# Splitting the SSD chunks by head group, and a new order of attention fill and output projection, in a hybrid layer kernel

## The chip, the cores and the metric

The kernel runs on one core of a Trainium2 chip. The metric is the device time of one execution in microseconds (us). Engines are named as the profile names them: PE is the matrix engine and PEld its weight loads, DVE the vector engine, ACT the scalar (activation) engine, POOL the general-purpose engine, and SP the engine that here only issues DMAs. Each engine works through its own instructions in order and waits on semaphores for the others. PE adds into PSUM, which is kept in banks of 128 x 512 float32; everything else lies in SBUF (128 partitions) or, between stages, in DRAM.

## The reference: what is computed

One layer over 2048 positions with model width 1024, in float32. Two mixers read the same normalised input, and one projection takes both back:

```
proj = rmsnorm(x) @ w_in              # q, k, v, z_sb, z_ssd, xBC, dt
q, k = rmsnorm per head (16 heads x 64)
z    = q k^T * scale                  # strictly causal
w    = exp(log_sigmoid(z) + sum over later keys of log_sigmoid(-z))
y_sb = rmsnorm((w @ v) * silu(z_sb), sb_norm_w)

xBC  = silu(causal_depthwise_conv(xBC, 4 taps))   # 12 blocks of 128 channels
y    = ssd_chunked(x*dt, dt*a, B, C)  # 16 heads, 2 B/C groups, chunks of 128
y_ssd = rmsnorm((y + D*x) * silu(z_ssd), ssd_norm_w)

out  = x + concat(y_sb, y_ssd) @ w_out
```

In the chunked scan each chunk of 128 positions makes a product inside the chunk (`C B^T` under a decay matrix `exp(a_t - a_s)`), one with the state carried in, and a new state `carry`. The heads of group 0 read B and C of group 0, those of group 1 of group 1; the groups share nothing else, and a chunk needs the state of the chunk before.

## The kernel before

**Stages.** The sequence is worked in two halves of 1024 positions (`H` = 0, 1), because a half of the normalised input fits in SBUF. In the order of the program: loading and splitting the input (to about 30 us), the four conv blocks of half 0 (to 145), SSD chunks and the SSD branch's gate projections of half 0 (to 385), attention for the queries of half 0 (to about 1010) and of half 1 (to about 2080), the conv blocks of half 1 (to 2195), its SSD chunks (to 2335), the output projection of the attention branch, called part 0 here (`br` = 0, to 2506), and of the SSD branch, part 1 (to 2702).

**Matmuls.** To keep float32 accuracy every operand is split into a rounded high part and the rest (`hh`, `hl`, `wh`, `wl`, `yh`, `yl`), and a product is made of three matmuls. A 128 x 512 block of a projection over the depth of 1024 is 8 x 3 = 24 matmuls of 512 columns. PSUM has eight banks under four tags: `z` 2, `t` 2, `av` 1, `pj` 3.

**SSD (`ssd`).** `conv(sg)` makes three of the twelve channel blocks: 144 matmuls in all, then for each block and half of 512 positions a copy from PSUM to `u` (ACT), the first tap with the bias (ACT), three taps (DVE, `scalar_tensor_tensor`), `Sigmoid` (ACT, into a buffer of `wk`) and a product (POOL). Blocks 0 to 2 come before block 3, which is called fourth here. `chunk(c)` makes both head groups of one chunk: transposes of x to `t`, `xd` (DVE) and `xdd` (POOL), the B/C product and its mask `cb` (DVE), for each of two quarters of heads a decay tile `wk`, also called `lm` (a broadcast DMA, four `Relu` and one `Exp` on ACT, a product with `cb` on POOL), the matmuls of L422 (inside the chunk) and L426 (with `carry`), two DVE operations into `ea` and one into x, the state matmul L434 and two DVE operations on `carry`. The gate projections `gates(wz, j, q)` are 24 matmuls each and depend on none of this. In half 0 all 16 blocks stand behind the chunks in the program; in half 1 the last four stand between chunks 0 and 1, chunks 2 and 3, and the rest (`CS` = (0, 2, 4)), together with the loading and splitting of `w_out` for part 0 (`load_wo`); the other twelve were made during attention.

**Attention (`attention`).** Sixteen segments per half: pairs of heads `p` and query halves `q` of 512 positions. For a segment, `stage_a` projects q, k and v and normalises q and k by rows, `stage_b` transposes them and makes the value differences `vd` (each value row less the one before), which the scan form of the stick-breaking weights needs, and `gate` the attention's gate. They are the fill: Python generators of small steps, from which a planner takes one whenever the inner loop of the current segment has saved up `UNIT` = 0.55 us of due time. That inner loop runs z (L610, L611), two ACT operations, the scan on DVE (L619), transposes (L628), a split and the value matmuls (L645, L646). `fill_for(n)` sets the fill's order while segment n runs.

**Output projection (`out_part`).** For each of 16 tiles of 128 positions: load the residual `res`, the branch `yr` and, in part 1, its gate `zr`; in part 1 two POOL products and a `Sigmoid` (L748 to L750); squares and their sum over the depth (`sq`, `sqs`, then a `ones` matmul, L757); a product with the norm's weight (POOL, L761); the split into `yh` (ACT, L762) and `yl` (DVE, L763); 48 matmuls, 24 for each half of 512 columns (L769 to L771); and the scaling by the row's norm with the residual added (L772), then a store. `yr` and `zr` have three buffers, `res` two.

**Order.** The program is written for a scheduler that places an instruction by its priority in the program and by when it can start, so that each engine's order isn't the order of the code; tiles of a pool wait for the last reader of the buffer that they take over.

Of the kernel before, what the change touches and what calls it, by code (L numbers as in the profile page):

```python
# [46 lines left out]
def hybrid_layer_kernel(ctx: ExitStack, tc: tile.TileContext, x, norm_w, wA, wP0, wP, wZ, wdt, vec, w_out, out):  # L47
# [9 lines left out]
    vb_d = nc.dram_tensor("vb_scr", [NP, P], F32).ap()  # L57
# [203 lines left out]
    def ssd(H, sp, wp, proj_t, proj_steps):  # L261
# [27 lines left out]
        XT = [X8[:, g, :] for g in range(8)] + [sp.tile([P, HALF], F32, name=f"XT{g}") for g in range(8, 12)]  # L289
        def conv(sg):  # L290
            wts = load_w(wp, wA[sg], wide=H == 0)

            both = H == 0 and sg == 0
            for gi, qs in ([(gi, (q,)) for q in range(2) for gi in range(3)] if both else
# [59 lines left out]
        conv(3)  # L354

        def chunks(c0, c1):
            if c0 == 0:
                sc.activation(dec, dec, AF.Exp)
                sc.activation(dte, dte, AF.Exp)
            for c in range(c0, c1):  # L360
                chunk(c)
            if c1 == 8:
                if H == 0:
                    nc.sync.dma_start(car_d, carry)
                for j in range(8):
                    nc.sync.dma_start(yss_d[j, :, H * HALF:(H + 1) * HALF], XT[j])

        def chunk(c):
            csl = slice(c * P, (c + 1) * P)

            xd = sp.tile([P, 16, 64], F32, name="xd", bufs=2)
            xdd = sp.tile([P, 16, 64], F32, name="xdd", bufs=2)
            for b in range(2):
                tp = ps("t")
                for j in range(4):
                    te.transpose(tp[:, j * P:(j + 1) * P], XT[b * 4 + j][:, csl], ident)
                hs = slice(c * 16 + b * 8, c * 16 + b * 8 + 8)
                ve.tensor_tensor(xd[:, b * 8:(b + 1) * 8, :], tp.rearrange("p (h d) -> p h d", d=64),
                                 dt[:, hs].unsqueeze(2).broadcast_to([P, 8, 64]), op=ALU.mult)
                gp.tensor_tensor(xdd[:, b * 8:(b + 1) * 8, :], xd[:, b * 8:(b + 1) * 8, :],  # L380
                                 dte[:, hs].unsqueeze(2).broadcast_to([P, 8, 64]), op=ALU.mult)

            for b in range(2):
                xg = X8[:, b * 4:b * 4 + 4, csl]
                gp.tensor_tensor(xg, xg, vt[:, V_D + b * 4:V_D + b * 4 + 4].unsqueeze(2).broadcast_to([P, 4, P]),
                                 op=ALU.mult)
            tp = ps("t")
            for g in range(2):
                te.transpose(tp[:, g * P:(g + 1) * P], XT[8 + g][:, csl], ident)
                te.matmul(tp[:, (2 + g) * P:(3 + g) * P], XT[8 + g][:, csl], XT[10 + g][:, csl],  # L390
                          start=True, stop=True)
            bn = sp.tile([P, 2, P], F32, name="bn", bufs=2)
            sc.copy(bn, tp[:, 0:256].rearrange("p (g n) -> p g n", g=2))
            cb = sp.tile([P, 2, P], F32, name="cb", bufs=2)
            ve.tensor_tensor(cb, tp[:, 256:512].rearrange("p (g n) -> p g n", g=2),
                             tri.unsqueeze(1).broadcast_to([P, 2, P]), op=ALU.mult)
            ea = sp.tile([P, 8, P], F32, name="ea", bufs=1)
            for par in range(2):
                src = acs_d[H, c * 16 + par, :]
                nc.sync.dma_start(ea[par * 64:(par + 1) * 64], bass.AP(  # L400
                    tensor=src.tensor, offset=src.offset, ap=[[0, 64], [2 * P, 8], [1, P]]))
            for b in range(2):
                sc.activation(ea[:, b * 4:(b + 1) * 4, :], ea[:, b * 4:(b + 1) * 4, :], AF.Exp)
            for g in range(2):
                yd = ps("z")
                yo = ps("z")
                for hq in range(2):
                    h0 = g * 8 + hq * 4
                    lm = sp.tile([P, 512], F32, name="wk", bufs=WKB).rearrange("p (i t) -> p i t", t=P)
                    src = acs_d[H, c * 16 + h0, :]  # L410
                    nc.sync.dma_start(lm, bass.AP(tensor=src.tensor, offset=src.offset,
                                                  ap=[[0, P], [P, 4], [1, P]]))
                    for i in range(4):
                        ac = acs[:, c * 16 + h0 + i:c * 16 + h0 + i + 1]
                        sc.activation(lm[:, i, :], lm[:, i, :], AF.Relu, scale=-1.0, bias=ac)
                    sc.activation(lm, lm, AF.Exp, scale=-1.0)
                    gp.tensor_tensor(lm, lm, cb[:, g, :].unsqueeze(1).broadcast_to([P, 4, P]), op=ALU.mult)
                    for i in range(4):
                        h = h0 + i
                        r0 = (i % 2) * 64  # L420
                        j = (h0 + i) // 2 - g * 4
                        te.matmul(yd[r0:r0 + 64, j * P:(j + 1) * P], xd[:, h, :], lm[:, i, :],  # L422
                                  start=True, stop=True)
                for j in range(4):
                    h = g * 8 + 2 * j
                    te.matmul(yo[:, j * P:(j + 1) * P], carry[:, h:h + 2, :], XT[10 + g][:, csl],  # L426
                              start=True, stop=True)
                eg = ea[:, g * 4:(g + 1) * 4, :]
                ve.tensor_tensor(eg, yo.rearrange("p (j t) -> p j t", t=P), eg, op=ALU.mult)
                ve.tensor_tensor(eg, yd.rearrange("p (j t) -> p j t", t=P), eg, op=ALU.add)  # L430
                xg = X8[:, g * 4:g * 4 + 4, csl]
                ve.tensor_tensor(xg, xg, eg, op=ALU.add)
                st = ps("av")
                te.matmul(st, bn[:, g, :], xdd[:, g * 8:(g + 1) * 8, :], start=True, stop=True)  # L434
                cg = carry[:, g * 8:(g + 1) * 8, :]
                ve.tensor_tensor(cg, cg, dec[:, c * 16 + g * 8:c * 16 + g * 8 + 8].unsqueeze(2)
                                 .broadcast_to([P, 8, 64]), op=ALU.mult)
                ve.tensor_tensor(cg, st.rearrange("p (h d) -> p h d", d=64), cg, op=ALU.add)
# [19 lines left out]
    def attention(ap_, wp, hp, hx):  # L458

        segs = [(H, p, q) for H in range(2) for p in range(NP) for q in range(2)]  # L460
        made, wts, wzs, rows, vrs, gzs = {}, {}, {}, {}, {}, {}
        hx1, nw1 = [], []

        def stage_a(H, p, q):

# [397 lines left out]
```

## Time and profile before

| | us |
|---|---|
| median of 3 runs | 2701.43 |
| lowest and highest | 2699.46 and 2707.42 |
| the profiled execution | 2703.41 |
| its span | 2701.6 |
| PE busy | 2569.6 (95%) |
| DVE busy | 1942.3 (72%) |
| ACT busy | 1609.5 (60%) |
| POOL busy | 887.9 (33%) |

The profile is of one execution, taken by the hardware. Its span runs from the first instruction to the last; 1.8 us of the execution lie around it. Busy times are sums over an engine's instructions, and "waits" are the idle time before an instruction, put down to what released it last. Matmul ends are modelled from their pipelining. The granted clock is that of PE as a share of full speed, 2.4 GHz.

### The profile page before, as it was taken

What the parts mean: (1) busy time and instruction counts of PE and PEld (TensorE: products, weight loads), DVE (VectorE), ACT (ScalarE), POOL (GpSimd) and SP (SyncE); (2) the same over time, 40 slices, a digit from 0 to 9 for tenths busy, and PEclk for the clock granted to TensorE, in tenths of its full rate; (3) what the DMA queues carried; (4) which work ended last, traced back from release to release, by engine and by line L of the source; (5) the groups of instructions that cost most, each with busy time, mean ns of one, the idle gap of its engine ahead of it and who ended that gap; (6) DMA issues with size and microseconds to landing.
All of it is one profiled execution on the core that took longest, in us unless ns stands there. A gap on an engine that the chain in (4) does not pass through costs nothing.

```text
span 2701.6 us, 40079 instructions
## 1 busy us (share of the span) xinstructions
PE 2569.6 (95%) x13858; PEld 2133.6 (79%) x13858; DVE 1942.3 (72%) x3002; ACT 1609.5 (60%) x3491; POOL 887.9 (33%) x876
## 2 busy tenths in 40 slices
PE   7989999999999999999999999999999996999989
PEld 5866788888888778787878888888776775778877
DVE  6557436666767677868686868688898766787666
ACT  4467436665666566868676767677887466332221
POOL 1468232323333222121212121212111568351553
PEclk9999999999999999999999999999999998999999
DMA  3125742333433422232323222223221136683553
GB/s 116 51 75 152 235 135 74 98 95 101 107 94 102 127 85 82 64 93 61 94 62 90 67 87 71 86 71 83 60 82 35 54 100 179 201 244 125 160 161 116
DMA packets 217867, 281.94 MB, mean 104 GB/s; under 512 B 20433, under 2 KB 129249, under 8 KB 217665
## 3 DMA queue, kind: packets, MB, share of 16 engines
q1 hardware_dynamic: 199232, 245.83, 31.4%
q10 hardware_dynamic: 18432, 33.56, 4.3%
q8 instruction: 109, 1.79, 0.3%
q14 instruction: 94, 0.76, 0.1%
HBM read 178.00 MB, written 59.38 MB: 88 GB/s over the span
## 4 chain that ended last, share of the span: by engine, by line
PE 61%; DVE 20%; ACT 6%; issue 6%; DMA 4%; POOL 3%; SPq 0%; DVEq 0%; ACTq 0%; POOLq 0%
DVE w L619 6%; PE t L628 5%; PE pj L483 5%; PE pj L482 5%; PE pj L481 5%; PE pj L250 4%; PE pj L251 4%; PE pj L249 4%; PE av L645 3%; PE z L610 3%; DVE tl L633 3%; PE z L611 3%; PE av L646 3%; PE pj L769 2%; PE pj L771 2%
## 5 line engine op out<-in xcount | busy, mean ns | idle before, releaser
L619 DVE TENSOR_TENSOR_SCAN w<-z,w,be 128x512 f32<-128x512 f32 x384 | 491.1, 1279 | 146.3 <-ACT z L616 144.7
L615 ACT ACTIVATE be<-z 128x512 f32<-128x512 f32 (+3 forms) x640 | 344.8, 539 | 351.9 <-PE z L611 176.5
L633 DVE TENSOR_TENSOR tl<-t,th 128x512 fp32r<-128x512 f32 (+3 forms) x640 | 377.4, 590 | 9.9 <-ACT th L631 9.0
L631 ACT CAST th<-t 128x512 fp32r<-128x512 f32 (+3 forms) x640 | 340.7, 532 | 33.7 <-PE t L628 31.6
L481 PE MATMUL pj<-wh,hh 128*128 128x384 f32 (+1 forms) x1024 | 349.3, 341 | 0.2 <-ACT hh L177 0.2
L628 PE MATMUL t<-ident,w 128*128 128x128 f32 x2176 | 344.8, 274 | 4.2 <-DVE tl L633 3.6
L483 PE MATMUL pj<-wh,hl 128*128 128x384 f32 (+1 forms) x1024 | 346.4, 338 | 0.0
L482 PE MATMUL pj<-wl,hh 128*128 128x384 f32 (+1 forms) x1024 | 346.1, 338 | 0.0
L616 ACT ACTIVATE z<-z 128x512 f32<-128x512 f32 (+3 forms) x640 | 343.2, 536 | 0.0
L619 DVE TENSOR_TENSOR_SCAN w<-z,be 128x128 f32<-128x128 f32 (+3 forms) x256 | 210.0, 820 | 177.6 <-ACT z L616 154.5
L137 POOL TENSOR_TENSOR wl<-wraw,wh 128x384 fp32r<-128x384 f32 (+3 forms) x163 | 169.3, 1049 | 421.2 <-ACT wh L136 413.5
L628 PEld LDWEIGHTS t<-ident,w 128*128 128x128 f32 x2176 | 258.0, 140 | 62.5 <-DVE tl L633 16.7
L653 POOL TENSOR_TENSOR y<-y,gz 64x512 f32<-64x512 f32 x64 | 82.9, 1295 | 509.0 <-DVE y L652 507.7
L481 PEld LDWEIGHTS pj<-wh,hh 128*128 128x128 f32 x1024 | 192.8, 188 | 12.6 <-ACT hh L177 0.7
L482 PEld LDWEIGHTS pj<-wl,hh 128*128 128x128 f32 x1024 | 192.7, 188 | 11.8
L483 PEld LDWEIGHTS pj<-wh,hl 128*128 128x128 f32 x1024 | 192.6, 188 | 0.7
L249 PE MATMUL pj<-hh,zh 128*128 128x512 f32 x432 | 175.3, 406 | 0.0
L250 PE MATMUL pj<-hl,zh 128*128 128x512 f32 x432 | 172.7, 400 | 0.0
L251 PE MATMUL pj<-hh,zl 128*128 128x512 f32 x432 | 172.3, 399 | 0.0
L645 PE MATMUL av<-th,V 128*128 128x512 f32 (+2 forms) x384 | 156.5, 408 | 9.5 <-DVE y L652 8.4
L610 PE MATMUL z<-M,AB 128*128 128x512 f32 (+2 forms) x384 | 140.5, 366 | 11.0 <-DVE w L619 8.9
L646 PE MATMUL av<-tl,V 128*128 128x512 f32 (+2 forms) x384 | 139.6, 364 | 0.0
(252 smaller groups left out, 5976.1 us busy)
## 6 DMA issues: line engine op xcount, KB each, us to landing
wraw<-in_wP_dram SPq DMA_DIRECT2D x112, 192.0 KB, 2.5
wk<-acs_scr SPq DMA_DIRECT2D x64, 256.0 KB, 4.2
M<-AB SPq DMA_DIRECT2D x128, 128.0 KB, 2.3
AB<-AB SPq DMA_DIRECT2D x128, 128.0 KB, 2.4
Mc<-kc_scr ACTq DMA_DIRECT2D x64, 256.0 KB, 2.6
Vc<-vc_scr ACTq DMA_DIRECT2D x64, 256.0 KB, 2.7
wraw<-in_wZ_dram SPq DMA_DIRECT2D x54, 256.0 KB, 2.6
wraw<-in_wA_dram SPq DMA_DIRECT2D x44, 192.0 KB, 2.4
```

Of the source, the lines that this page charges most:

```text
L249: te.matmul(pj[:m], a, hh[q][:, kt, :], start=(kt == 0), stop=False)
L250: te.matmul(pj[:m], a, hl[q][:, kt, :], start=False, stop=False)
L251: te.matmul(pj[:m], b, hh[q][:, kt, :], start=False, stop=(kt == KT - 1))
L481: te.matmul(pj[:, :n], a, wh[kt][:, 0:n], start=(kt == 0), stop=False)
L482: te.matmul(pj[:, :n], a, wl[kt][:, 0:n], start=False, stop=False)
L483: te.matmul(pj[:, :n], b, wh[kt][:, 0:n], start=False, stop=(kt == KT - 1))
L615: sc.activation(be[:, :nk], zp[:, :nk], AF.Sigmoid, scale=0.125)
L616: sc.activation(zp[:, :nk], zp[:, :nk], AF.Sigmoid, scale=-0.125)
L619: ve.tensor_tensor_scan(w[:, 0:nk][:, ::-1], zp[:, 0:nk][:, ::-1], be[:, 0:nk][:, ::-1], 0.0 if diag else prev[i][:, 0:1], ALU.mult, ALU.add)
L628: te.transpose(tp[:, i * P:(i + 1) * P], ws[i][:, j * P:(j + 1) * P], ident)
L631: sc.copy(th[:, rs], tp[:, rs])
L633: ve.tensor_tensor(tl[:, rs], tp[:, rs], f32(th[:, rs]), op=ALU.subtract)
```

## The change

**Attention.** The row norm of a segment with q = 1 leaves `stage_a` and becomes `norm_rows`, called through `normed` while the next segment's fill is made; for q = 0 it stays where it was. The value differences leave `stage_a` for `stage_b` (`differences`). The last value row of each earlier block now goes through DRAM (`vb_d`, 24 rows instead of 8) where for part of the segments it was copied from SBUF. In half 1, for q = 0 and p below 6, 28 steps of the next `stage_a` run before `stage_b` and the rest behind it (12 before).

**SSD.** `chunk(c, g)` makes one head group. The fourth conv block became a generator, `conv_steps(3)`, worked half by half on the PSUM tag `pj`; one step of it is taken behind each chunk of group 0, and its sigmoids are collected to its end (`silu`). `chunks(c0, c1)` makes group 1 alone.

**Output projection.** The norm's weight is multiplied into `w_out` in `load_wo`, so L761 is gone. `prepare(t + 1)` stands ahead of the matmuls of tile t. The `yl` matmuls come behind all others of a half, and the `ones` matmul behind the first half.

```
         def conv_steps(sg):
...
+            both = sg == 3 or H == 0 and sg == 0
...
-                pjs = {q: ps("pj" if g % 2 else "z") for q in qs}
+                pjs = {q: ps("pj" if g % 2 or sg == 3 else "z") for q in qs}
...
-                    sg_ = sp.tile([P, 512], F32, name="wk", bufs=WKB)
-                    sc.activation(sg_, xc, AF.Sigmoid)
-                    gp.tensor_mul(xc, xc, sg_)
+                    raw_x.append(xc)
+                    if sg != 3:
+                        silu(raw_x)
+                yield
+            silu(raw_x)
...
-        conv(3)
-        def chunk(c):
-            xd = sp.tile([P, 16, 64], F32, name="xd", bufs=2)
+        def chunk(c, g):
+            xd = sp.tile([P, 8, 64], F32, name="xd", bufs=4)
...
+        last = conv_steps(3)
+        for c in range(8):
+            chunk(c, 0)
+            next(last, None)
+        drain(last)
         def chunks(c0, c1):
             for c in range(c0, c1):
-                chunk(c)
+                chunk(c, 1)
...
+            if q == 0:
+                norm_rows(H, p, q)
+            if 2 * H + q < 3:
+                nc.sync.dma_start(vb_d[2 * H + q, p:p + 1, :], vr[P - 1:P, 3, :])
...
         def stage_b(H, p, q):
-            vd, raw = rows.pop((H, p, q))
+            vr, raw, _ = rows.pop((H, p, q))
+            vd = differences(H, p, q, vr)
...
                 rest = stage_a(*nn)
-                for _ in range(NA if n else 0):
+                first = 28 if H == 1 and q == 0 and p < NJ else NA if n else 0
+                for i in range(first):
+                    if i == first - 4:
+                        normed(nx)
                     next(rest)
                     yield
+            normed(nx)
+            if first == 28:
+                yield from rest
...
         def load_wo(op, k0, n, hl, raw_, br):
-                sc.copy(h[:, c:c + 512], raw)
-                (ve if k % 2 else gp).tensor_sub(l[:, c:c + 512], raw, f32(h[:, c:c + 512]))
+                w = vt[:, off + k:off + k + 1]
+                if k % 2:
+                    sc.activation(h[:, c:c + 512], raw, AF.Copy, scale=w)
+                    ve.scalar_tensor_tensor(l[:, c:c + 512], raw, w, f32(h[:, c:c + 512]), ALU.mult, ALU.subtract)
+                else:
+                    sc.activation(raw, raw, AF.Copy, scale=w)
+                    sc.copy(h[:, c:c + 512], raw)
+                    gp.tensor_sub(l[:, c:c + 512], raw, f32(h[:, c:c + 512]))
...
-            gp.tensor_tensor(yr, yr, vt[:, off:off + 8].unsqueeze(2).broadcast_to([P, 8, P]), op=ALU.mult)
+        ahead = [prepare(0)]
+        for t in range(SEQ // P):
+            if t + 1 < SEQ // P:
+                ahead.append(prepare(t + 1))
+            res, yh, yl, sqs = ahead.pop(0)
...
                     te.matmul(acc, yh[:, k, :], wl[k][:, cs], start=False, stop=False)
+                for k in range(8):
                     te.matmul(acc, yl[:, k, :], wh[k][:, cs], start=False, stop=(k == 7))
+                if ch == 0:
+                    mp = ps("t")
+                    te.matmul(mp[:, 0:2], sqs, ones[:, 0:2], start=True, stop=True)
```

ACT, first half, end of the fourth conv block, before (`X_384` is the x block, L306 the copy to `u`, L309 the first tap, L314 the sigmoid, L136 the split of gate weights, L415 and L416 `Relu` and `Exp` of the decay tile, L393 the copy of B):

```order
L314 ACTIVATE wk<-X_384 128x512 x2
L393 COPY bn<-t 128x256
L415 ACTIVATE wk<-wk,acs 128x128 x5
L416 ACT_TABLE_LOAD
L416 ACTIVATE wk<-wk 128x512
L415 ACTIVATE wk<-wk,acs 128x128 x4
L416 ACTIVATE wk<-wk 128x512
L415 ACTIVATE wk<-wk,acs 128x128 x4
L416 ACTIVATE wk<-wk 128x512
```

The same place now (L293 is the sigmoid, L318 and L321 copy and first tap, L389 the copy of B, L397 the `Exp` for `ea`):

```order
L293 ACT_TABLE_LOAD
L293 ACTIVATE wk<-X_384 128x512
L397 ACT_TABLE_LOAD
L397 ACTIVATE ea<-ea 128x512
L293 ACT_TABLE_LOAD
L293 ACTIVATE wk<-X_384 128x512 x3
L136 CAST wh<-wraw 128x384
L318 COPY u<-pj 128x512
L136 CAST wh<-wraw 128x384
L321 ACTIVATE X_384<-u,vt 128x512
L389 COPY bn<-t 128x128
L136 CAST wh<-wraw 128x256
```

Before, the last sigmoids stand together ahead of the first `Relu`; now they alternate with the chunks' `Exp`, and a table load stands at each change between them.

PE, second half, from the last chunk to the first output tile, before (L422, L426 and L434 are the chunk's matmuls, L376, L389 and L390 its transposes and B/C product, L769 to L771 the output's):

```order
L434 MATMUL av<-xdd,bn 128x512
L376 MATMUL t<-ident,X_23761 128x128 x4
L434 MATMUL av<-xdd,bn 128x512
L376 MATMUL t<-ident,X_23761 128x128 x4
L769 MATMUL pj<-hh_25155,yh 128x512
L770 MATMUL pj<-hl_25156,yh 128x512
L769 MATMUL pj<-hh_25155,yh 128x512
L770 MATMUL pj<-hl_25156,yh 128x512
L771 MATMUL pj<-hh_25155,yl 128x512
L769 MATMUL pj<-hh_25155,yh 128x512
L770 MATMUL pj<-hl_25156,yh 128x512
L422 MATMUL z<-wk,xd 64x128 x8
```

The same place now (L414, L418 and L424 are the chunk's matmuls, L386 and L387 its B transpose and B/C product, L808 and L809 the output's):

```order
L424 MATMUL av<-xdd,bn 128x512
L386 MATMUL t<-ident,XT_23859 128x128
L387 MATMUL t<-XT_23861,XT_23859 128x128
L414 MATMUL z<-wk,xd 64x128 x8
L418 MATMUL z<-XT_23861,carry 128x128 x4
L424 MATMUL av<-xdd,bn 128x512
L414 MATMUL z<-wk,xd 64x128 x8
L424 MATMUL av<-xdd,bn 128x512
L418 MATMUL z<-XT_23861,carry 128x128 x4
L808 MATMUL pj<-hh_25619,yh 128x512
L809 MATMUL pj<-hl_25620,yh 128x512
```

Before, output matmuls stand among those of the last chunk; now all of the chunks' stand ahead of the first output matmul.

SP, part 1 of the output projection, two tiles of its regular run, before (numbers tell buffers and tiles apart: `res` of a tile is 266 below the `yr` and 532 below the `zr` in the same round, which belong to later tiles):

```order
L744 DMA yr_27693<-yss_scr 128x8x128
L742 DMA res_27427<-res_scr 128x1024
L773 DMA out_0_dram<-res_27339 128x512
L747 DMA zr_27959<-gss_scr 128x8x128
L773 DMA out_0_dram<-res_27339 128x512
L744 DMA yr_27781<-yss_scr 128x8x128
L742 DMA res_27515<-res_scr 128x1024
```

The same place now:

```order
L780 DMA yr_27882<-yss_scr 128x8x128
L778 DMA res_27619<-res_scr 128x1024
L783 DMA zr_28145<-gss_scr 128x8x128
L817 DMA out_0_dram<-res_27532 128x512 x2
L780 DMA yr_27969<-yss_scr 128x8x128
L778 DMA res_27706<-res_scr 128x1024
L783 DMA zr_28232<-gss_scr 128x8x128
L817 DMA out_0_dram<-res_27619 128x512 x2
```

Before, one store of a tile stands ahead of the `zr` load and one behind it; now both stand between the `zr` load and the next `yr` load.

## Rows read from the trace of the kernel before

**Rows 1.** The page: busy time of each engine, share of the span, instructions

```profile
PE 2569.6 (95%) x13858; PEld 2133.6 (79%) x13858; DVE 1942.3 (72%) x3002; ACT 1609.5 (60%) x3491; POOL 887.9 (33%) x876
```

**Rows 2.** Busy times by stage: us, engines (instructions), TensorE clock, DMA share, GB/s

```profile
145.00:200.00 55.00, 47.18 (x227) 36.88 (x227) 28.89 (x37) 35.16 (x68) 33.08 (x41) 0.98 0.25 75
200.00:300.00 100.00, 93.79 (x611) 68.70 (x609) 69.77 (x94) 66.99 (x178) 68.36 (x55) 1.00 0.57 163
...
1010.00:2080.00 1070.00, 1036.06 (x5756) 858.10 (x5756) 860.73 (x1224) 791.16 (x1699) 198.85 (x231) 1.00 0.27 75
...
2195.00:2335.00 140.00, 111.61 (x690) 81.75 (x689) 98.39 (x141) 87.58 (x214) 104.45 (x82) 0.93 0.55 156
2335.00:2506.00 171.00, 166.26 (x744) 135.05 (x742) 129.54 (x226) 44.43 (x51) 55.48 (x29) 0.99 0.63 199
2506.00:2702.00 196.00, 182.36 (x801) 146.91 (x799) 133.61 (x239) 41.11 (x42) 98.00 (x39) 0.99 0.47 144
```

**Rows 3.** Waits of PE, 2195 to 2335: us in total, times, longest

```profile
PE z L422 <- POOL wk L417: 8.1, 5, 2.6
PE z L422 <- DVE ea L429: 7.8, 3, 6.0
PE pj L769 <- ACT yh L762: 5.8, 1, 5.8
```

**Rows 4.** Waits of PE, 1010 to 2080

```profile
PE z L610 <- DVE w L619: 22.6, 66, 1.5
```

**Rows 5.** Waits of PE, 2506 to 2702

```profile
PE pj L771 <- DVE yl L763: 8.4, 6, 1.9
PE pj L769 <- ACT yh L762: 0.8, 1, 0.8
```

**Rows 6.** Timeline, 2561.5 to 2576: start, us, engine, line, operation, tiles

```profile
2561.64 2.88 POOL L761 TENSOR_TENSOR yr<-yr,vt 128x1024 f32<-128x1024 f32 x1
...
2562.27 0.28 PE L757 MATMUL t<-ones,sqs 128*128 128x2 f32 x2
...
2562.79 0.39 SPq L744 DMA_DIRECT2D yr<-yss_scr  x1
...
2568.56 2.40 POOL L748 TENSOR_TENSOR yr<-yr,zr 128x1024 f32<-128x1024 f32 x1 [4.04 <-DMA yr<-yss_scr]
...
2573.55 0.28 PE L757 MATMUL t<-ones,sqs 128*128 128x2 f32 x2
...
2574.57 0.37 SPq L747 DMA_DIRECT2D zr<-gss_scr  x1
2574.99 0.57 SPq L773 DMA_DIRECT2D out_dram<-res  x1
...
2575.65 0.39 SPq L744 DMA_DIRECT2D yr<-yss_scr  x1
```

**Rows 7.** PE by line and form, 200 to 300: xcount, busy, mean ns, idle before

```profile
L426 PE MATMUL z<-XT,carry 128*128 128x128 f32 x112 | 16.3, 287 | 0.8 <-DVE ea L430 0.7
```

**Rows 8.** Busy times of the tile `pj` alone, 200 to 300

```profile
200.00:300.00 100.00, 50.76 (x169) 31.11 (x167) 0.00 (x0) 4.56 (x8) 1.00 0.57 163
```

**Rows 9.** Timeline of ACT, from 148 to 167

```profile
148.35 1.28 ACT L358 ACT_TABLE_LOAD   x1
149.64 0.31 ACT L358 ACTIVATE dec<-dec 128x128 f32<-128x128 f32 x1
...
151.26 0.63 ACT L314 ACTIVATE wk<-X 128x512 f32<-128x512 f32 x1
...
166.15 0.51 ACT L136 CAST wh<-wraw 128x384 fp32r<-128x384 f32 x1 [0.15 <-PE pj L250]
```

**Rows 10.** Busy times of a q = 1 and a q = 0 segment

```profile
1498.30:1565.50 67.20, 65.47 (x369) 53.62 (x368) 59.87 (x87) 55.38 (x119) 14.53 (x17) 1.00 0.24 66
1565.50:1635.30 69.80, 67.78 (x381) 58.31 (x379) 47.63 (x71) 44.81 (x97) 11.96 (x14) 1.00 0.31 88
```

**Rows 11.** The page: DMA issues, KB each, median us to landing

```profile
M<-AB SPq DMA_DIRECT2D x128, 128.0 KB, 2.3
```

More of the change, by code (lines that the diff above doesn't have):

```diff
@@ L289, in ssd, with silu, conv_steps @@
         XT = [X8[:, g, :] for g in range(8)] + [sp.tile([P, HALF], F32, name=f"XT{g}") for g in range(8, 12)]
+        def silu(xs):
+            for xc in xs:
+                sg_ = sp.tile([P, 512], F32, name="wk", bufs=WKB)
+                sc.activation(sg_, xc, AF.Sigmoid)
+                gp.tensor_mul(xc, xc, sg_)
+            xs.clear()
         def conv(sg):
+            drain(conv_steps(sg))
+        def conv_steps(sg):
             wts = load_w(wp, wA[sg], wide=H == 0)
-            both = H == 0 and sg == 0
+            raw_x = []
+            both = sg == 3 or H == 0 and sg == 0
             for gi, qs in ([(gi, (q,)) for q in range(2) for gi in range(3)] if both else
@@ L366, in chunks @@
                     nc.sync.dma_start(yss_d[j, :, H * HALF:(H + 1) * HALF], XT[j])
-        def chunk(c):
-            csl = slice(c * P, (c + 1) * P)
-            xd = sp.tile([P, 16, 64], F32, name="xd", bufs=2)
[L372 to L438, printed above, removed]
@@ L460, in attention @@
         segs = [(H, p, q) for H in range(2) for p in range(NP) for q in range(2)]
-        made, wts, wzs, rows, vrs, gzs = {}, {}, {}, {}, {}, {}
-        hx1, nw1 = [], []
+        made, wts, wzs, rows, gzs = {}, {}, {}, {}, {}
+        hx1, nw1, done = [], [], set()
         def stage_a(H, p, q):
@@ L494, in stage_a, with norm_rows, differences @@
                     add_bias(xdt1[:, (q * 4 + t) * 16:(q * 4 + t + 1) * 16], pj[:, 384:400])
+            rows[H, p, q] = (vr, raw, ss)
+            if q == 0:
+                norm_rows(H, p, q)
+            if 2 * H + q < 3:
+                nc.sync.dma_start(vb_d[2 * H + q, p:p + 1, :], vr[P - 1:P, 3, :])
+        def norm_rows(H, p, q):
+            _, raw, ss = rows[H, p, q]
+            r = rsqrt(ap_, ss.rearrange("p t g -> p (t g)"), 16, 1.0 / 64, "qk")
+            rv = raw.rearrange("p t (g d) -> p (t g) d", d=64)
+            ve.tensor_tensor(rv, rv, r.unsqueeze(2).broadcast_to([P, 16, 64]), op=ALU.mult)
+        def differences(H, p, q, vr):
             vd = ap_.tile([P, 4, P], F32, name="vd", bufs=1)
@@ L570, in gates1, with normed @@
                 nc.sync.dma_start(gss_d[j, :, t0:t0 + 512], zr)
+        def normed(seg):
+            if seg[2] == 1 and seg not in done:
+                norm_rows(*seg)
+                done.add(seg)
         def fill_for(n):
@@ L578, in fill_for @@
                 yield from gate(*nx)
-            rest = iter(())
+            rest, first = iter(()), 0
             if n + 2 < len(segs):
@@ L725, in load_wo @@
     def load_wo(op, k0, n, hl, raw_, br):
+        off = V_SSW if br else V_SBW
         for k in range(k0, k0 + n):
@@ L738, in out_part, with prepare @@
         n = 0
-        for t in range(SEQ // P):
+        def prepare(t):
             tsl = slice(t * P, (t + 1) * P)
```

86 lines of the change are left out of this document (66 added, 20 removed).

## The prediction

> **What bounds the kernel now.** I read the engines' shares first: PE is busy for 95% of the span [rows 1], so only its 132 us without work (2701.6 − 2569.6) and its pace can be won. The stage table then tells where they are [rows 2]: subtract PE's busy time from the length of each stretch. The chunks of the second half stand out: 28.4 us of 140 (140.00 − 111.61), with a mean granted clock of 0.93. The chunks of the first half lose 7.8 us in 145 to 200 and 6.2 in 200 to 300; attention over the second half 33.9 of 1070; the output projection 4.7 (171 − 166.26) in its attention part and 13.6 (196 − 182.36) in its SSD part. Third, the waits of those stretches. In the second half's chunks PE waits for POOL's product `wk` and DVE's `ea`, and 5.8 us once for `yh` of the first output tile [rows 3]. In attention it waits 66 times for the scan `w`, 22.6 us in all [rows 4]. In the SSD part of the projection it waits for `yl` and `yh`, 9.2 us [rows 5].
>
> Two paces serve throughout. An output tile, from `ones` matmul to `ones` matmul, takes 2573.55 − 2562.27 = 11.28 us when PE has all it needs [rows 6]; it holds 48 matmuls 512 columns wide, so one costs 0.235 us. One chunk of one head group, below a unit, holds eight `carry` matmuls; 112 in 200 to 300 [rows 7] make 14 units, beside 169 gate and projection matmuls [rows 8]. PE's part of a unit is thus (93.79 − 169 × 0.235)/14 = 3.86 us; DVE's, ACT's and POOL's, at most, 69.77, 66.99 and 68.36 over 14: 4.98, 4.8 and 4.9 [rows 2]. So a unit alone is limited by its side engines, 1.1 us beyond PE, and some five wide matmuls beside it cover that.
>
> **The change, part by part.** The sum is made against the profiled execution, 2703.4 us, which is 2.0 above the median 2701.4.
>
> *First half, chunks.* Group 0 of all chunks now runs beside the 144 matmuls of the fourth conv block. PE: 8 × 3.86 + 144 × 0.235 = 64.7 us. DVE: 8 × 4.98, and for the conv at most the 28.9 that it was busy in 145 to 200 [rows 2]: 68.7. ACT in the same way 8 × 4.8 + 35.2 = 73.6. Side engines and PE are about equal, so how much stays uncovered is a matter of order. Comparable stretches idled 6% (200 to 300) and 20% (2195 to 2335): 4 to 14 us, of which I take 8, nearer to the first because a conv block has as many matmuls for eight units as that stretch had for seven. The group 1 stretch then has 8 × 4.98 = 40 us of DVE against 8 × 3.86 + 34 × 0.235 = 39 of PE (34 gate matmuls stand among them in the new order), some 6 us. Before: 7.8 + 6.2 = 14.0. Change 0, between −6 and +8.
>
> The conv's sigmoids, collected to its end, land on ACT between Exp operations of the chunks. ACT loads tables 11 times a half where it did 5 times. One load costs 1.28 us and the next function began 0.01 us behind it: 148.35 to 149.64 [rows 9]. Six loads now stand in one row of ACT's order (171 to 191), with five sigmoids at 0.63 and four casts at 0.51 [rows 9], 5.2 us, and other short operations that I put at as much again: 6 × 1.28 + 10.4 = 18 us without the next `wk`. PE has there about 14 wide matmuls and one unit, 7 us. Whether up to 11 or 12 us show per half depends on whether PE is still behind when ACT comes to this row. By the totals above (PE must issue 34 us of conv first, sigmoids need the conv's end, which PE itself delivers) I take it that nearly all is covered and put 2 us, inside the 8; uncovered it is a rival.
>
> Here a rule speaks against the change, and the row against the rule. The Trainium skill, "ScalarE: Activation LUTs", section "What ACT_TABLE_LOAD costs", adds a drain of about 1.38 us to each load of 1.28, 2.66 a switch. The trace does not agree: with 0.01 us between load and function [rows 9] there is no room for a drain behind the load. The twelve additional loads are 15 us of ACT's time by the row. They would be an estimated 32 by that section.
>
> *Second half, chunks.* The same split. After: 8 for group 0; 2 for the four chunks of group 1 that have gate blocks between them; the last four units are bare, 4 × (4.98 − 3.86) = 4.5; ahead of them ACT has nine scalings and casts of `w_out`, at 0.51 for such a cast [rows 9], 4.6 us; and 1 at the change to the output. That is 20 against 28.4. In this stretch 7% of the clock were missing over 111.6 us of busy time, 7.8 us; with a third less idle time I give back 3 of it. Change −8 − 3 = −11, between −21 (the idle time falls to 10) and +3 (group 0 as in the 20% case, bare units twice as dear).
>
> *Attention.* The norm of the q = 1 rows moves into the q = 0 segment. A q = 1 segment over the second half has DVE busy 59.87 of 67.2 us with 87 operations, a q = 0 one 47.63 of 69.8 with 71 [rows 10]. Twelve of 87 operations leave the crowded one, 14%; of 22.6 us of waiting for the scan [rows 4] that is 3 us. Both ends: −11, if half the waits go, and +5, if the q = 0 segments, denser by the same twelve, begin to wait as the others did (2 us more in two or three of them). The value differences, moved to `stage_b`, now depend on rows that came a segment earlier; their DMAs land in about 2.3 us, as `AB` and `M` do [rows 11], against a segment of 67, so the extra pass through DRAM costs nothing. Were that cover gone, each of 24 would stand open for 2.3 us. Change −3.
>
> *Output projection.* Folding the norm weight into `w_out` takes POOL's `tensor_tensor` off each tile: 2.88 us in a row of L761 [rows 6]. It was never the last thing before PE, and its additional ACT work (eight scalings a part) lies where ACT is busy 44 us of 171 [rows 2]. The tile prepared ahead and the `yl` matmuls at the end of each half take away the waits of the attention part: 4.7 to about 2, −3. The SSD part is bound otherwise, by a loop through SP: load of `yr` issued at 2562.79, its gate product at 2568.56 (5.77 for issue and data), sigmoid, second product, and only then is a `zr` buffer free: 2574.57; behind it in SP's queue one store, then the next `yr` at 2575.65. The period is 2575.65 − 2562.79 = 12.86 us against PE's 11.28, and the six waits are its price [rows 5, 6]. Order and buffers of `zr` remain, and now both stores stand between `zr` and `yr`. One more store is 0.57 of SP: 13.4. If its 256 KB delay the data as well, by the like again, 13.9; if the store's issue falls beside another wait, 12.86 − 0.57 = 12.3. Nine tiles hang on it (4 to 12, whose loads stand behind a `zr` that must come free): 9 × 0.54 = +4.9, from 9 × (12.3 − 12.86) = −5.0 to 9 × 1.04 = +9.4. The loop begins a little earlier, since the first tile is prepared before the weights of this part are done; I give that 1 us, an estimate. Change −3 + 4.9 − 1 = +1, between −8 and +6.
>
> Sum: 0 − 11 − 3 + 1 = −13 from 2703.4, that is 2690.4; less the 2.0 between this execution and the median, 2688.
>
> **Rivals.**
> B, the covers hold nearly everywhere: first half −4, second −21, attention −11, output −8. Sum −44: 2657. For it: the group split halves what a unit must wait for. Against: side engines equal to PE's time in the group 0 stretch.
> C, the gain is eaten: group 0 as in the 20% stretch (+6 and, in the second half, −5), loop at 13.9 (+6), attention −3. Sum +4: 2705.
> D, on the other side: the row of six table loads isn't covered. ACT reaches it early, PE runs through its 7 us and waits 11 to 12, in both halves: +24 on the forecast, 2712. It decides if the last sigmoid starts less than about 18 us before PE would need the next `wk`. For it: the order; against: five sigmoids can't start before PE has issued the conv.
> E, each load holds ACT about twice as long as its row, because the engine stands still ahead of it until its work has drained: six loads as long again, 6 × 1.28 = 7.7 more per half on top of D, 2727. The rows [rows 9] speak against it. It is the rule of the Trainium skill, "ScalarE: Activation LUTs", section "What ACT_TABLE_LOAD costs".
>
> **How the numbers follow.** About 0.3%, 8 us, can be told from no change: faster is below 2693.3, slower above 2709.5. Forecast A (2678 to 2698): 0.45, of it 0.36 faster, 0.09 same. B 0.15, faster. C 0.27, of it 0.03 faster, 0.19 same, 0.05 slower. D 0.11: 0.02 same, 0.09 slower. E 0.02, slower. Sums: faster 0.54, same 0.30, slower 0.16. The range 2658 to 2712 leaves out half of B (0.07), half of D (0.05) and E: 0.14, with the tails of A and C about 0.2.
>
> **What the profile after would show.** Right: idle time of PE between 2195 and the output near 20 us with a clock above 0.95; no wait of more than 3 us for `wk` around the last sigmoid; fewer waits for `w` in q = 1 segments; no wait for `yl` in the attention part, and `yr` issues 13.4 us apart in the SSD part. Wrong: a gap of about 10 us after the conv block (D), a load loop at 11.3 (B), or more waits for `w` in q = 0 segments than q = 1 lost.

## The result: slower, and where the profile after puts it

The changed kernel takes 2724.17 us (median of 4 runs, 2720.21 to 2726.19) against 2700.44 for the kernel before in the same comparison: a ratio of 1.0077, 95% interval 1.0059 to 1.0095. It is slower by 21 us (by the ratio) to 24 us (by the medians), where 2688 and a gain were forecast; the time lies above the range, 2658 to 2712. The profiled execution's span is 2724.0.

Busy times by stage in the changed kernel (us; PE, PEld, DVE, ACT, POOL with instructions; clock; DMA share; GB/s). The stages are the first half's group 0 and group 1 stretches, the second half's chunks, and the output's parts 0 and 1:

```profile
141.00:230.00 89.00, 72.00 (x409) 53.15 (x407) 59.76 (x81) 64.78 (x139) 62.87 (x58) 0.96 0.32 95
230.00:300.00 70.00, 61.57 (x395) 44.31 (x394) 41.17 (x64) 46.96 (x129) 45.40 (x37) 1.00 0.69 216
...
2177.00:2346.00 169.00, 134.62 (x766) 98.02 (x765) 103.00 (x145) 118.02 (x267) 113.20 (x99) 0.91 0.49 142
2346.00:2535.00 189.00, 187.42 (x843) 155.45 (x842) 130.97 (x269) 55.97 (x64) 31.37 (x16) 1.00 0.60 190
2535.00:2724.00 189.00, 174.27 (x758) 141.24 (x757) 92.54 (x225) 38.37 (x39) 57.30 (x24) 0.98 0.44 142
```

Against [rows 2]: PE lacks 17.0 us in the group 0 stretch and 8.4 in the group 1 stretch, where the chunks of the first half lacked 14.0 before; in the second half's chunks 34.4 instead of 28.4, with a clock of 0.91 instead of 0.93. In part 0 of the output only 1.6 are left of 4.7, in part 1 14.7 stand against 13.6. By marks in the program: attention, counted from its first `z` matmul to its last, begins at 399.0 instead of 384.0, 15.0 later; it takes 1678.2 instead of 1679.8; from its end to PE's last matmul pass 642.6 instead of 633.4. The loss is in the two SSD stages.

Not all of the 15.0 us are idle time. From 141 to the start of attention, before and then now:

```profile
141.00:384.04 243.04, 228.23 (x1284) 183.50 (x1283) 120.59 (x177) 134.87 (x325) 124.24 (x117) 0.99 0.49 148
```
```profile
141.00:399.00 258.00, 232.58 (x1284) 184.80 (x1283) 114.91 (x185) 142.52 (x339) 131.96 (x117) 0.99 0.46 139
```

PE idles 25.4 us instead of 14.8, which is 10.6 of the 15.0; in the other 4.4 it is busy for longer with as many matmuls; what slows them isn't shown.

What PE waits for in the first half's chunks, 141 to 300 (us in total, times, longest):

```profile
PE z L414 <- POOL wk L410: 16.7, 19, 2.1
PE av L424 <- POOL xdd L380: 5.2, 4, 2.0
```

And one unit of group 0 there, from its timeline (start, length, engine, line; in brackets the idle time before and what ended it):

```profile
189.16 0.60 PE L377 MATMUL t<-ident,X 128*128 128x128 f32 x4
...
189.84 1.04 POOL L383 TENSOR_TENSOR X<-X,vt 128x512 f32<-128x512 f32 x1 [3.81 <-PE t L377]
...
191.35 0.68 DVE L378 TENSOR_TENSOR xd<-t,dt 128x512 f32<-128x512 f32 x1
...
192.11 1.48 POOL L380 TENSOR_TENSOR xdd<-xd,dte 128x512 f32<-128x512 f32 x1 [0.64 <-DVE xd L378]
...
193.55 3.38 POOL L410 TENSOR_TENSOR wk<-wk,cb 128x512 f32<-128x512 f32 x2
193.64 1.13 PE L424 MATMUL av<-xdd,bn 128*128 128x512 f32 x2 [1.23 <-POOL xdd L380]
...
195.31 0.66 PE L414 MATMUL z<-wk,xd 128*64 128x128 f32 x8 [0.55 <-POOL wk L410]
...
196.98 0.66 PE L414 MATMUL z<-wk,xd 128*64 128x128 f32 x8 [1.01 <-POOL wk L410]
```

POOL is idle for 3.81 us until PE transposes, and then PE is idle, three times, until POOL has made `xdd` and two `wk`. Neither engine is full in this stretch (PE is busy for 72.00 and POOL for 62.87 of its 89 us); each unit closes a chain over both. By its state matmuls (L424) this unit stands 10.6 us behind the one before and 11.0 ahead of the next, where PE's own work in one, with 18 conv matmuls, is 3.86 + 18 × 0.235 = 8.1.

### The profile page after: what moved, and what is told of

The parts are those of the page before. It is cut to its first block, busy times and chain, and to the rows that moved or that the text cites. A ratio compares the mean times of both kernels' runs of the same rounds, so it can differ in the third digit from the quotient of the medians.

```text
span 2724.0 us, 40128 instructions
## 1 busy us (share of the span) xinstructions
PE 2578.5 (95%) x13858; PEld 2144.4 (79%) x13858; DVE 1883.1 (69%) x3018; ACT 1635.2 (60%) x3535; POOL 817.6 (30%) x844
## 4 chain that ended last, share of the span: by engine, by line
PE 63%; DVE 13%; ACT 7%; issue 6%; POOL 5%; DMA 4%; SPq 1%; ACTq 0%; DVEq 0%; POOLq 0%
PE t L655 6%; PE pj L490 5%; PE pj L489 5%; PE pj L488 5%; DVE w L646 5%; PE pj L251 5%; PE pj L250 5%; PE pj L249 5%; PE z L637 4%; PE av L672 3%; PE z L638 3%; PE av L673 3%; DVE tl L660 2%; PE pj L808 2%; PE pj L809 2%
```

## Experiments: which of the three edits

The change was taken apart: each group of edits alone on the kernel before, and the two others without the SSD edits.

> The kernel before with the SSD edits alone (group split, fourth conv block interleaved, its sigmoids at its end). Theory S: the split of the chunks is the whole loss, +15 in the first half (attention begins at 399.0 instead of 384.0) and +14 in the second; the other edits give about 7 back: 2729. Theory T (the loss comes from edits acting together, as the output's order behind all chunks): about 2700 to 2710.


Measured 2736.4 us, ratio 1.0136 (1.0116 to 1.0156).

> The kernel before with the attention edits alone. From begin to end of attention the changed kernel took 1.6 us less: 2699 by theory S. By theory T no statement; if the deferred norms cost where the SSD edits don't cover them, 2705.


Measured 2697.0, ratio 0.9978 (0.9966 to 0.9989).

> The kernel before with the output projection's edits alone. Theory S: tiles at 11.13 instead of 11.28 (32 x 0.15 = 4.8 us) and the load loop at 13.5 instead of 12.9 (+5), waits of the attention part less by 5: 2695. Theory T: the gain needs the new SSD order, 2701.


Measured 2704.4, ratio 1.0010 (0.9998 to 1.0022): no difference that can be told.

> The changed kernel with its SSD edits undone (attention and output edits stay). Theory S: both small gains, 2693, 31 us below the changed kernel. Theory T: 2700 to 2710.


Measured 2696.5, ratio 0.9977 (0.9965 to 0.9990); the kernel before had 2702.8 in these four comparisons. So the SSD edits are the whole loss: 33.6 us alone, 27.7 beside the others (2724.2 − 2696.5). The attention edits gain 5.8 (e2). The kernel before measured 2700.4 to 2704.4 in the different comparisons, so a difference between kernels of two comparisons is uncertain by about as much. In the changed kernel's attention, from 1010 to 2080, PE waits 15.1 us in 53 times for the scan, where [rows 4] has 22.6 in 66:

```profile
PE z L637 <- DVE w L646: 15.1, 53, 0.8
```

## Experiments: what in the SSD edits

First the deferred sigmoids and their table loads. Code from here on is shortened, with comments added; `D`, `gate` and `pool` stand for longer expressions.

```
-            silu(raw_x)
+            silu(raw_x, AF.Exp)        # e5: Exp instead of Sigmoid
...
-                    if sg != 3:
-                        silu(raw_x)
+                    silu(raw_x)        # f2: each sigmoid behind its own half
```

> The changed kernel with the fourth conv block's Sigmoid replaced by Exp (so that block's values aren't the reference's): 16 of the 25 table loads vanish, PE's order stays the same until the block's last sigmoids. Theory D (the table loads are the loss): all of the 22 us come back, 2701. Theory L (PE and POOL wait for each other once a unit, because a unit's transposes stand only 3 to 7 matmuls ahead of its state matmul): only the stalls around the last sigmoids come back, 216 to 223 in the first half, 4.7 us and the lower clock behind them, about 5 a half: 2714.


Measured 2741.2, ratio 1.0140: 17 us slower than the changed kernel, with 16 table loads fewer. Taking these loads away doesn't bring the loss back, and theory L, which expected 10 us back, missed as well. The changed kernel's POOL shows what stands at the place that the prediction feared:

```profile
205.11 2.94 POOL L410 TENSOR_TENSOR wk<-wk,cb 128x512 f32<-128x512 f32 x2
208.01 6.47 POOL L294 TENSOR_TENSOR X<-X,wk 128x512 f32<-128x512 f32 x4
214.44 1.01 POOL L137 TENSOR_TENSOR wl<-wraw,wh 128x384 fp32r<-128x384 f32 x1
215.41 1.38 POOL L383 TENSOR_TENSOR X<-X,vt 128x512 f32<-128x512 f32 x1
...
220.93 2.48 POOL L410 TENSOR_TENSOR wk<-wk,cb 128x512 f32<-128x512 f32 x2
```

The sigmoids' four products, 6.47 us, and six other operations stand in POOL's order ahead of the next `wk` product, which comes 13 us after the last one; ACT itself is idle for 3.25 us in that time. PE's waits for `wk` there are 2.1 us at the longest. Why the kernel with Exp is slower than the changed one isn't settled; its clock in 200 to 230 was 0.84 against 0.94 there.

> The changed kernel with the fourth conv block's sigmoids where those of the other blocks are, each behind its own block half; the rest stays. 29 table loads instead of 25, but no row of sigmoids. If the run of deferred sigmoids (POOL's five products L294 in a row ahead of the next wk, and ACT's loads) costs, the gaps at 216 to 223 and the low clock behind them go, 5 to 8 us a half: 2712. If table loads as such cost, 4 more at 1.28: 2729.


Measured 2711.1, ratio 1.0029 (1.0018 to 1.0039): 13 us back, with four table loads more.

Then the chain over POOL, by an earlier head and by less work on POOL:

```
+            if c < 7:
+                head(c + 1, 0)         # e6: ahead of the conv step
             next(last, None)
...
-            gp.tensor_tensor(xg, xg, D, op=ALU.mult)
-            ve.tensor_tensor(xg, xg, eg, op=ALU.add)
+            for j in range(4):         # e7: x*D + y on DVE
+                ve.scalar_tensor_tensor(xg[:, j, :], xg[:, j, :], D[j], eg[:, j, :], ALU.mult, ALU.add)
```

> The changed kernel with the head of the next chunk (transposes, xd, xdd, B/C product) written ahead of the conv step instead of behind it; in PE's order 14 to 24 conv matmuls then stand between a unit's transposes and its state matmul, instead of 5, for the later half of the group 0 stretch; the group 1 stretch is as it was; 21 table loads. Theory L: the waits for xdd and wk in the group 0 stretch go in those units, 4 units at 2.5 us a half and the run of loads covered: 2708. Theory D: 2720.


Measured 2724.8, ratio 1.0079: nothing. With up to 24 conv matmuls between two units' state matmuls PE waited for `wk` less often but longer (5.5 us at most instead of 2.1), 25.8 us idle from 141 to the start of attention against 25.4. Theory L falls as far as the place of the head goes.

> The changed kernel with POOL's product of x and D (L383) taken into DVE's last addition of a unit (four scalar_tensor_tensor of 128 columns in place of one addition of 512). POOL loses 1.04 us a unit, and the transposed x needn't wait for it. Theory L: 1 us off each of 32 units' chains, nearly all of it on PE's path in the group 0 stretches and half of it in the group 1 stretches: 2700. Theory D: only 17 loads instead of 25, 2715. If DVE becomes the limit instead (0.5 us more a unit): 2720.


Measured 2718.5, ratio 1.0058 (1.0041 to 1.0075): 6 us of the 24 expected, and its interval overlaps that of the changed kernel (1.0059 to 1.0095), so that even these 6 aren't clear of noise.

Then the split itself, in the old order of chunks:

> The changed kernel with its chunk code split by head group but in the old order: the fourth conv block whole and first, with its own sigmoids, then for each chunk group 0 and group 1. Theory L (order, not splitting, is the loss): 2696, as the kernel with the SSD edits undone. Rival G (the split has a price of its own, more small operations and waits a unit): 2705 or more.


Measured 2719.8, ratio 1.0061 (1.0046 to 1.0076). The conv block beside group 0 and the deferral are both gone, and the loss is nearly all there: rival G.

> As the kernel with the chunk code split in the old order (2720), but the heads of both groups (transposes, xd, xdd, B/C product) written ahead of both tails, as the code before had them. Theory P: the split costs because a group's head no longer stands a whole group's work ahead of its tail; with it back, 2697. Theory M: what costs is the doubled number of small operations and buffers (two more PSUM tiles of tag t, two ea loads, two bn copies a chunk), which this keeps: 2718.


Measured 2718.4, ratio 1.0051: it isn't the place of the heads.

> The split in the old order with the fourth conv block as the code before had it (blocks whole, tags z and pj). If the conv's halves cost, 2697. Theory W (units without wide matmuls among them are limited by their side engines): its order has 0 to 3 wide matmuls between most units and 133 behind the last in the first half, so as slow as the others or slower, 2722.


Measured 2724.1, ratio 1.0077 (1.0062 to 1.0092): nor the conv block's halves, which these kernels had kept. Splitting the chunk code alone costs about 27 us against the kernel with the SSD edits undone (e4).

What the split brings along is a line that neither the description nor the prediction spoke of: `ea`, one tile for both groups in one buffer, became a tile for one group in two buffers. g2 and g3 change this number alone, in the changed kernel and in g1:

```
-            eg = sp.tile([P, 4, P], F32, name="ea", bufs=2)
+            eg = sp.tile([P, 4, P], F32, name="ea", bufs=1)
```

> The changed kernel with one ea buffer instead of two, nothing else. In the order, 5 to 12 wide matmuls stand before each unit of group 1 instead of 1 to 3, and 6 to 16 before those of group 0. Theory W: the group 1 stretches lose 2 us instead of 8, the group 0 stretches some 5 less, in both halves about 20 together: 2704. If the split's own small operations cost (theory M), or the single buffer makes units wait, 2724 or more.


Measured 2713.4, ratio 1.0040 (1.0025 to 1.0055): 11 us back.

> The split in the old order, conv as before, with one ea buffer: 7 to 12 wide matmuls stand before each state matmul and each wk matmul. Theory W: 2697, as the kernel with the SSD edits undone (2696.5). Theory M: 2718.


Measured 2694.7, ratio 0.9972 (0.9963 to 0.9981): 29 us below g1, in the same comparison, by one buffer less. Attention begins at 388.5 in it and at 404.7 in g1. This is theory W, and its mechanism can be read from both profiles. In 200 to 300, all engines and then the tile `pj` alone (gate and projection matmuls), g1:

```profile
200.00:300.00 100.00, 75.23 (x528) 52.48 (x525) 75.46 (x104) 63.30 (x178) 66.49 (x52) 0.97 0.58 180
```
```profile
200.00:300.00 100.00, 20.65 (x61) 11.71 (x62) 0.00 (x0) 1.15 (x2) 0.97 0.58 180
```

and g3:

```profile
200.00:300.00 100.00, 92.31 (x585) 66.86 (x585) 67.01 (x90) 62.51 (x172) 71.33 (x57) 1.00 0.45 139
```
```profile
200.00:300.00 100.00, 53.89 (x186) 33.44 (x186) 0.00 (x0) 4.57 (x8) 1.00 0.45 139
```

With two buffers 61 wide matmuls run in this stretch, with one 186, and 169 before [rows 8]. From one unit's state matmuls to the next stand two or three of them in g1 (218 to 273) and 12 to 18 in g3. PE idles 24.8 us with two buffers and 7.7 with one. The waits in the same stretch, g1 and then g3:

```profile
PE z L413 <- POOL wk L409: 14.4, 17, 1.4
PE pj L249 <- ACT zr L446: 8.6, 1, 8.6
```
```profile
PE av L423 <- DVE carry L426: 5.3, 7, 1.3
PE t L376 <- DVE cb L390: 0.9, 1, 0.9
```

The order explains itself so, by the code: with one buffer the next unit's `ea` load has to wait for the unit before, and in the order that the scheduler lays out the gate matmuls come forward into that gap; with two, units stand close together and the gates lie behind them, where nothing waits. The counts and waits are measured; the scheduler's choice is argued.

A unit with so few wide matmuls is paced by its chain over the side engines. In g1 ten units, by their state matmuls from 218.26 to 277.66, are 5.9 us apart with 21 wide matmuls among them; PE's own work is 3.86 + 2.1 × 0.235 = 4.35 us in each. DVE is busy for 56.59 of 65 us there, PE for 50.35:

```profile
218.26 1.02 PE L423 MATMUL av<-xdd,bn 128*128 128x512 f32 x2
...
277.66 1.02 PE L423 MATMUL av<-xdd,bn 128*128 128x512 f32 x2
```
```profile
215.00:280.00 65.00, 50.35 (x378) 34.94 (x374) 56.59 (x79) 46.90 (x134) 52.33 (x42) 1.00 0.48 133
```

What remains in g2 was told apart by two more kernels; h3 is shown against g3.

> The changed kernel with one ea buffer and its fourth conv block's sigmoids each behind its own half. If the two losses are separate, 2724 less 13 less 11: 2700. If both edits act by spreading the same wide matmuls, 2710. If the conv block beside group 0 costs nothing by itself, 2695.


Measured 2715.7, ratio 1.0043 (1.0030 to 1.0056). With one buffer the deferred sigmoids cost nothing (2713.4 with them), so the 13 us of f2 and the 11 of g2 don't add: either edit takes back what the other would.

```
+        for c in range(8):
+            chunk(c, 0)
         def chunks(c0, c1):
             for c in range(c0, c1):
-                chunk(c, 0)
                 chunk(c, 1)
```

> The split with one ea buffer, the fourth conv block whole and ahead as in the code before, then all chunks of group 0 and then all of group 1. If the conv block beside group 0 costs the remaining 21 us (its copies, taps, sigmoids and products come on top of the units' work on ACT, DVE and POOL, where gate matmuls bring one ACT copy in 24), 2695. If the order by groups costs it, because each unit waits for the carry of the unit next to it, 2715.


Measured 2698.3, ratio 0.9988 (0.9978 to 0.9998). The order by groups costs 4 us at most (2694.7 in g3); the conv block beside group 0 costs the other 17 (2715.7 − 2698.3; 15 by the ratios). Between h1 and h3 the block's halves and PSUM tags change too, which brought no gain from e8 to g1. A conv block's 144 matmuls bring six copies, taps, sigmoids and products, 18 DVE operations among them, to engines that a unit already keeps busy (DVE for 56.59 of the 65 us in g1), while 24 gate matmuls bring one ACT copy. That this is why it costs was not shown by a run of its own.

## Experiments: the loop of the output's SSD part

The loop is there as forecast. SP in part 1 of the changed kernel:

```profile
2571.20 0.42 SPq L780 DMA_DIRECT2D yr<-yss_scr  x1
2575.40 0.33 SPq L778 DMA_DIRECT2D res<-res_scr  x1
2583.13 0.37 SPq L783 DMA_DIRECT2D zr<-gss_scr  x1
2583.61 0.99 SPq L817 DMA_DIRECT2D out_dram<-res  x2
2584.69 0.45 SPq L780 DMA_DIRECT2D yr<-yss_scr  x1
```

The period is 13.49 us, forecast 13.4, against 12.86 before [rows 6]. Three kernels tried to open it.

```
-                nc.sync.dma_start(zr, gate)          # f3, g4
+                nc.scalar.dma_start(zr, gate)
...
-            yr = pool.tile(..., name="yr", bufs=3)   # g4; zr 3 -> 2
+            yr = pool.tile(..., name="yr", bufs=4)
...
-                sc.activation(zr, zr, AF.Sigmoid)    # h2, on g3; zr 3 -> 2
+                sg = ow.tile([P, 8, P], F32, name="sg", bufs=1)
+                sc.activation(sg, zr, AF.Sigmoid)
```

> The kernel with attention and output edits but the old SSD (2696.5), its zr loads of part 1 issued by ACT instead of SP. ACT's Square of the same tile already waits for what the zr load waits for, and the loads of yr no longer queue behind it. If the loop through SP's queue is what part 1 loses (its tiles 7 to 12 take 13 to 15 us instead of 11.13), they fall to 11.13: 12 us less, 2685. If the loss is the data rate of the loads or POOL's products, 2696.


Measured 2696.0, ratio 0.9971, against 2696.5 without it: nothing. Its timeline shows the loop closed elsewhere:

```profile
2575.05 0.38 SPq L773 DMA_DIRECT2D yr<-yss_scr  x1
...
2579.22 2.40 POOL L777 TENSOR_TENSOR yr<-yr,zr 128x1024 f32<-128x1024 f32 x1 [7.01 <-DMA yr<-yss_scr]
...
2581.65 1.06 ACT L778 ACTIVATE zr<-zr 128x1024 f32<-128x1024 f32 x1 [7.96 <-DMA out_dram<-res]
...
2585.22 0.37 ACTq L776 DMA_DIRECT2D zr<-gss_scr  x1
2585.63 1.04 ACT L786 CAST yh<-yr 128x1024 fp32r<-128x1024 f32 x1 [1.97 <-POOL yr L779]
...
2586.78 1.22 DVE L787 TENSOR_TENSOR yl<-yr,yh 128x1024 fp32r<-128x1024 f32 x1 [6.53 <-ACT yh L786]
2588.03 0.38 SPq L773 DMA_DIRECT2D yr<-yss_scr  x1
```

`yr` needs a buffer that `yl` of an earlier tile frees; its `yh` stands in ACT's order behind the Sigmoid of the tile just loaded, and now behind the `zr` issue too, which waits for the second product. The period is 12.98. The expectation had the `zr` issue wait for nothing that ACT didn't wait for anyhow; it was moved from one in-order queue into another that holds the same loop.

> The kernel with attention and output edits, old SSD, zr loads on ACT (2696.0), with four yr buffers and two zr buffers. There the loop went on at 12.95 us a tile: yr load, first product, Sigmoid, Square of the tile before and yh of the tile before that in ACT's order, yl, and then the yr buffer. With one tile more of yr the loop closes a tile later: tiles at 11.13 all through, 9 to 10 us less, 2686. If the loads' data rate is the limit, 2696.


Measured 2697.5, ratio 0.9981: nothing. The order used the fourth buffer to start the gate of a tile one tile earlier; `yh` still stands behind the newest Sigmoid, and tiles still take 12.9.

> The split in the old order with one ea buffer (2694.7), the output's Sigmoid written to a tile of its own (zr keeps two buffers instead of three), so that it needs zr alone. The loop of 13.5 us a tile in part 1 then has no link from a yr load to the yh of an earlier tile over ACT's order. If that link closes the loop, tiles at 11.13 and 12 to 17 us less: 2680. If the loads' rate or POOL's products are the limit, 2695.


Measured 2688.0 (four runs, 2679.6 to 2692.7), ratio 0.9939 (0.9918 to 0.9960), against 2694.7 and 0.9972 for g3. Five tiles still take 12.0 to 12.9 us, so the loop is shorter and begins later but isn't gone: `sg` has one buffer, and ACT waits for its second product before the next Sigmoid. This kernel is faster than both, by 16 us against the kernel before in its comparison (2704.4) and by 36 against the changed one.

## Why the prediction was wrong, point by point

*First half, chunks: 0 forecast, −6 to +8; +15.0 in the profile.* This step failed. The group 0 stretch was put at 8 us of idle time between 4 and 14, "nearer to the first"; it had 17.0. The reason given for the choice, as many wide matmuls for eight units as 200 to 300 had for seven, misread the row: 169 for 14 units are 12 a unit, 144 for eight are 18. There was more cover by count, and it covered less. What the runs showed in its place is a chain: PE waits 16.7 us for `wk` and 5.2 for `xdd`, both made by POOL, and no engine is full (in the 89 us DVE is busy for 59.76, ACT 64.78, POOL 62.87, PE 72.00). The forecast weighed totals of DVE and ACT against PE's and formed none for POOL; in the same way it would have been 8 × 4.9 + 33.1 = 72 us against PE's 64.7. With gates beside the units instead, 10 to 14 a unit in the same order by groups, the loss is gone (h3, with one `ea` buffer; attention begins at 384.6). That the conv block's own side work makes it load instead of cover fits this, and is argued. The 4.4 us of longer busy time had no term at all. The group 1 stretch, 8.4 against 6, was near.

*Second half, chunks: −11 forecast, −21 to +3.* This step failed too, and in its direction. From the end of attention to the end of the span the changed kernel takes 2724.0 − 2077.2 = 646.8 us in its profiled execution; e4, which differs from it by the SSD edits alone, takes 2687.9 − 2052.1 = 635.8, so the step is about +11. e1 (2735.3 − 2085.1 = 650.2) against the kernel before (2701.6 − 2063.8 = 637.8) gives +12.4. Idle time in the chunks was put at 20 us and is 34.4, and no clock came back. The same causes are at work as far as the profiles tell; here only four gate blocks exist as cover, and the last three units, to their state matmuls at 2343.83, have no wide matmul between them:

```profile
2320.67 2.05 PE L424 MATMUL av<-xdd,bn 128*128 128x512 f32 x2 [3.81 <-ACT bn L389]
```
```profile
2320.00:2346.00 26.00, 19.33 (x120) 13.30 (x121) 18.74 (x25) 15.93 (x40) 20.77 (x17) 0.75 0.64 191
```

A bare unit was put at 4.98 us from a stretch where gates ran beside it. These three take 7.7 each, at a mean clock of 0.75, and just ahead of them PE waits 3.81 us for ACT's copy of B; in g1, at full clock and with two wide matmuls in each, they take 5.9, 1.6 beyond PE's own work instead of 1.1.

*What was missed altogether.* The second `ea` buffer, worth 29 us in the split alone and 11 in the changed kernel. The forecast counted 34 gate matmuls in the new order among the group 1 units and took that number as given, without asking what had put 169 among 14 units before.

*Table loads.* No drain, as the rows said. One switch in the changed kernel:

```profile
195.60 0.39 ACT L408 ACTIVATE wk<-wk,acs 128x128 f32<-128x128 f32 x1
196.06 1.28 ACT L293 ACT_TABLE_LOAD   x1
197.36 0.63 ACT L293 ACTIVATE wk<-X 128x512 f32<-128x512 f32 x1
```

The work ahead of the load ends at 195.99, 0.07 us before it, and the Sigmoid begins 0.02 us behind it. Rival E, the rule of the Trainium skill, "ScalarE: Activation LUTs", section "What ACT_TABLE_LOAD costs", is not borne out here. That its 2727 lies nearest to the measured time is luck. Rival D named the right place, the collected sigmoids, which f2 shows to cost 13 us beside two `ea` buffers, but not what happens there: its gap of some 10 us isn't in the profile, e5 without these loads was slower, and f2 with four more was faster.

*Attention: −3 forecast.* By the edits alone −5.8 (−9 to −3 by the interval); −1.6 in the profiled execution. The step holds in direction: waits for the scan fell by 7.5 us, and those for `tl` rose by 1.4 (1.4 to 2.8).

*Output: +1 forecast, −8 to +6.* The loop's period, 13.4, was right to 0.1. Part 0 kept 1.6 us instead of 2. Not foreseen was that a tile takes 11.13 instead of 11.28 us, 32 × 0.15 = 4.8 us in all. With −3.1 in part 0 and +1.1 in part 1 that would make about −7, but alone these edits made no difference (e3). So the +1 agrees with e3 in the sum and partly by luck; where the 7 us went wasn't found.

## What to carry to other kernels

Before matmuls of one kind are given to a stretch as cover, count what they bring to the other engines, and follow one unit's chain instead of comparing totals: here matmuls that end in one copy per 24 covered a unit, and those that end in a filter and an activation did not. And in a program whose order a scheduler lays out, a buffer count is an ordering statement: here one buffer more left two or three wide matmuls between units instead of 12 to 18, so the first thing to compare after such a rewrite is how many covering instructions stand between two units. And moving a wait out of one in-order queue gained nothing here, because the queue that it was moved into lay on the same loop.

## What the runs showed that was not expected

The output's tile pace went from 11.28 to 11.13 us with the same matmuls, in every kernel with the output edits; whether the `yl` matmuls at the end of a half or the place of the `ones` matmul does it was not tried. Attention with the same code took 1669 to 1681 us in the profiled executions of different kernels, more than its own edits changed, so the stage's difference between two single profiles says little. Each edit also lets the scheduler lay out the whole order anew, so a difference of a few us between two kernels can't be put down to the edited line by its time alone; the 29 us of the buffer are far beyond that. And two losses that looked separate, 13 us for the deferral and 11 for the buffer, did not add: with the buffer repaired the deferral cost nothing.
